# A decoder layer's mixer: diagonal and lowest HGRN scores by products and ones matmuls, narrow stationary operands at level 64, and mLSTM score matmuls of two heads in turn

## The chip, the cores and the metric

The kernel runs on one core of a Trainium2 chip. Its parts here are TensorE (PE in the profile; PEld is its weight load), VectorE (DVE), ScalarE (ACT), GpSimd (POOL) and SyncE (SP, which issues the DMAs). The metric is the time of one execution in device microseconds. Before the change it is 960.95 us, the median of 3 runs (960.86 to 961.06).

## The reference

One decoder layer on 512 tokens of width 1024, in float32: a SwiGLU feed-forward block, a token mixer, and a second SwiGLU block, each between RMS norms with a residual. The mixer has four HGRN2 heads (128 wide) and four mLSTM heads (q and k 64 wide, values 128 wide). The part that this change touches is how scores are formed.

```
# HGRN, per head: G is the running sum of log f, k = 1 - f
scores[t, s] = sum_d q[t, d] * k[s, d] * exp(G[t, d] - G[s, d])      for s <= t
o = scores @ v + (q * exp(G)) @ state
# mLSTM, per head
P[t, s] = (q[t] . k[s]) * exp(D[t, s] - m[t])                         for s <= t
```

On the diagonal (s = t) the HGRN decay is 1 and the score is sum_d q k. For neighbours (t odd, s = t - 1) it is sum_d q[t] f[t] k[s], because one step of decay is f[t] = 1 - k[t].

## The kernel before, in words

Activations lie transposed, features on partitions and tokens along the free axis, so a matmul contracts over features. Precision comes from splitting each float32 operand in a high and a low part in the fp32r format and adding three products (hi·hi, hi·lo, lo·hi): lines L126 to L128, L433, L443 and L488 are these dense products. ScalarE makes the high part of each weight block (`split`, L208), VectorE the low part (L210). Four such blocks stand ready ahead of TensorE (`WBUF`), and each load of a raw block waits until an earlier one has been split.

The mixer lies between about 360 and 640 us. Its small score matmuls are float32 and stand between pieces of the big projections: `fill(n)` takes n pieces from a list of jobs (six 256-column matmuls of `job_f`, or three 512-column matmuls of `job_t`), so that TensorE has work while ScalarE and VectorE prepare the next operands. Instructions of each engine run in the order in which they were placed; that order is fixed when the program is built.

HGRN heads are handled in two pairs (p = 0, 1). Within blocks of 128 tokens the scores are formed by levels: at level c (64, 32, 16, 8, 4, 2, 1) a block of 2c tokens is cut in half, rows of the later half are multiplied with columns of the earlier half, both scaled with decays taken from the token at the cut. `hgrn_level` makes qe and ke on VectorE (L995, L996, L1003) and ScalarE (L997, L998), does 8 matmuls with 128 stationary and 64 moving columns (L1008), and writes the masked part of the result into the score tile sT (L1012, a predicated copy on VectorE). The lowest level, c = 1, needs no exponential: qe is q times 1 - k (L1000, L1003), and the stationary operand is k itself. `hgrn_diag` forms the diagonal from 8 matmuls of 128 by 128 (L1048), of which one entry in 128 is kept by a predicated copy through an identity mask (L1050). `hgrn_levels` sets the order: lowest level and diagonal first, then `hgrn_decays` (L956 to L968, which overwrites k by G - ln k), then the levels from 64 down. The matmul at L1008 for level 64 therefore comes after k has been overwritten and exponentiated.

`mlstm_scores` runs over the four mLSTM heads. For each, a matmul with a selector of 36 rows (L1148, `neg_m`) spreads the running maximum over the partitions, VectorE and ScalarE form the exponent (L1170 to L1173), GpSimd cuts it to the causal part, and four matmuls (L1182) of 64 rows form q·k. Heads 0 and 2 lie in partitions 0 to 63 of their tile, heads 1 and 3 in partitions 64 to 127. L1184 multiplies the two.

A float32 matmul shows as two rows of PE and two of PEld in the profile: the 8 matmuls of a level are 16 loads.

Names in the tile list that matter below: `st` is a ring of four 128x512 tiles shared by qe, el, e and others; `gpre` and `gpost` are 128x1024 tiles that hold the gains of the norms, loaded by SP when free; `xn` is a 128x1024 tile used in turn for several things; `ps` are the eight PSUM banks.

Of the kernel before, what the change touches and what calls it, by code (L numbers as in the profile page):

```python
# [67 lines left out]
class Layer:  # L68
# [814 lines left out]
    def masks(self, mc, mb):  # L883

        nc = self.nc

        self.mask = mb.tile([P, len(LEVELS), 64], I32, name="mask")
        nc.gpsimd.memset(self.mask, 1)
        for n, c in enumerate(LEVELS):
            m = self.mask[:, n, :].rearrange("p (b c) -> p b c", c=c)  # L890
            pat = [[-2 * c, 64 // c], [0, c]]
            nc.gpsimd.affine_select(m, m, pattern=pat, compare_op=ALU.is_ge, fill=0.0, base=0, channel_multiplier=1)
            pat = [[2 * c, 64 // c], [0, c]]
            nc.gpsimd.affine_select(m, m, pattern=pat, compare_op=ALU.is_ge, fill=0.0, base=c - 1, channel_multiplier=-1)
        self.eye = mb.tile([P, P], I32, name="eye")
        nc.gpsimd.memset(self.eye, 1)
        nc.gpsimd.affine_select(
            self.eye, self.eye, pattern=[[1, P]], compare_op=ALU.is_equal, fill=0.0, base=0, channel_multiplier=-1
        )

        sel = mb.tile([4, 6, 2, 64], F32, tag="tmp", bufs=1, name="sel")
        nc.gpsimd.memset(sel, 1.0)
        self.sel = mc.tile([36, 6, P], F32R, name="selr")
        nc.gpsimd.memset(self.sel.bitcast(I32), 0)
        for n in range(6):
            pat = [[0, 2], [0, 64]] if n < 4 else [[-1, 2], [0, 64]]
            base = -n if n < 4 else -2 * (n - 4)
            nc.gpsimd.affine_select(
                sel[:, n], sel[:, n], pattern=pat, compare_op=ALU.is_equal, fill=0.0, base=base, channel_multiplier=1
            )  # L910
        for r in (0, 32):
            nc.gpsimd.tensor_copy(self.sel[r : r + 4], sel.rearrange("p n a b -> p n (a b)"))
# [32 lines left out]
            self.G.append(G)  # L945
            self.fill(4)

    def st(self, name, n=512):
        return self.sp.tile([P, n], F32, tag="st", bufs=4, name=self.nm(name))

    def hgrn_decays(self, p):

        nc = self.nc
        G, H = self.G[p], self.kk[p]

        nc.scalar.activation(H, H, AF.Ln, bias=self.tiny)  # L956
        nc.vector.tensor_tensor(H, G, H, op=ALU.subtract)
        chunks = lambda t: t.rearrange("p a (c t) -> p (a c) t", c=NT)
# [7 lines left out]
        d = self.sp.tile([P, 2, T], F32, tag="xn", bufs=1, name=self.nm("ek"))  # L966
        nc.vector.tensor_tensor(chunks(d), end.broadcast_to([P, 8, P]), chunks(H), op=ALU.subtract)
        nc.scalar.activation(d, d, AF.Exp)  # L968
        return d

    def hgrn_edges(self, p, d):
# [4 lines left out]
        for a in range(2):  # L976
# [2 lines left out]
                nc.tensor.transpose(pt[:, c * P : (c + 1) * P], d[:, a, c * P : (c + 1) * P], self.ident)  # L979
            nc.scalar.copy(self.kdt[:, 2 * p + a, :], pt[:, : 3 * P])  # L980

    def hgrn_level(self, p, n, ke):

        nc = self.nc
        c = LEVELS[n]
        q, kk, G = self.q[p], self.kk[p], self.G[p]
        flat = lambda t: t.rearrange("p a t -> p (a t)")
        blk = lambda t: flat(t).rearrange("p (b two c) -> p b two c", two=2, c=c)
        qe = self.st("qe")
        qe3 = qe.rearrange("p (b c) -> p b c", c=c)  # L990
        if c > 1:
            el = self.st("el")
            el3 = el.rearrange("p (b c) -> p b c", c=c)
            ref = blk(G)[:, :, 0, c - 1 : c].broadcast_to([P, 512 // c, c])
            nc.vector.tensor_tensor(qe3, blk(G)[:, :, 1, :], ref, op=ALU.subtract)  # L995
            nc.vector.tensor_tensor(el3, ref, blk(kk)[:, :, 0, :], op=ALU.subtract)  # L996
            nc.scalar.activation(qe, qe, AF.Exp)  # L997
            nc.scalar.activation(blk(ke)[:, :, 0, :], el3, AF.Exp)  # L998
        else:
            nc.vector.tensor_scalar(qe3, blk(kk)[:, :, 1, :], -1.0, 1.0, op0=ALU.mult, op1=ALU.add)  # L1000
            ke = kk
        yield
        nc.vector.tensor_tensor(qe3, qe3, blk(q)[:, :, 1, :], op=ALU.mult)  # L1003
        yield
        sc = self.ps()
        k8, q8 = flat(ke).rearrange("p (n s) -> p n s", s=P), qe.rearrange("p (n u) -> p n u", u=64)
        for m in range(8):
            nc.tensor.matmul(sc[:, 64 * m : 64 * m + 64], k8[:, m], q8[:, m], start=True, stop=True)  # L1008
        yield
        so = self.sT[:, 8 * p : 8 * p + 8, :].rearrange("p n (b two c) -> p n b two c", two=2, c=c)[:, :, :, 1, :]  # L1010
        mk = self.mask[:, n : n + 1, :].broadcast_to([P, 8, 64]).rearrange("p n (b c) -> p n b c", c=c)
        nc.vector.copy_predicated(so, mk, sc.rearrange("p (n b c) -> p n b c", n=8, c=c))  # L1012
        yield

    def hgrn_levels(self, p, kes, per, then=lambda: None):

        L = [self.hgrn_level(p, n, kes[n % 2]) for n in range(len(LEVELS))]
        N = len(L)
        next(L[0])
        next(L[0])  # L1020
        self.hgrn_diag(p)
        self.fill(per // 2)
        next(L[0])
        d = self.hgrn_decays(p)
        self.fill(per // 2)
        next(L[1])
        next(L[0])
        self.fill(per)
        for n in range(1, N):
            if n == 2:  # L1030
                self.hgrn_edges(p, d)
                then()
            if n + 1 < N:
                next(L[n + 1])
            next(L[n])
            if n > 1:
                next(L[n - 1])
            self.fill(per)
            next(L[n])
        next(L[N - 1])  # L1040

    def hgrn_diag(self, p):
        nc = self.nc
        for a in range(2):
            sc = self.ps()
            for c in range(NT):
                s = slice(c * P, (c + 1) * P)
                nc.tensor.matmul(sc[:, s], self.kk[p][:, a, s], self.q[p][:, a, s], start=True, stop=True)  # L1048
            h = 2 * p + a
            nc.vector.copy_predicated(  # L1050
                self.sT[:, 4 * h : 4 * h + 4, :], self.eye[:, None, :].broadcast_to([P, NT, P]), sc.rearrange("p (n s) -> p n s", s=P)
            )

    def hgrn_states(self):

# [107 lines left out]
    def mlstm_head(self, h):  # L1163

        nc = self.nc
        nm = self.neg_m(h)
        nm4 = nm.rearrange("p (c t) -> p c t", c=NT)
        e = self.st("e")
        e4 = e.rearrange("p (c t) -> p c t", c=NT)
        nc.vector.tensor_tensor(e4, nm4, self.aT[:, :, h : h + 1].broadcast_to([P, NT, P]), op=ALU.add)  # L1170
        nc.vector.tensor_copy(self.nend[:, h, :].rearrange("p (c o) -> p c o", o=1), nm4[:, :, P - 1 : P])
        nc.vector.tensor_scalar(e, e, 0.0, None, op0=ALU.min)
        nc.scalar.activation(e, e, AF.Exp)  # L1173
        nc.gpsimd.affine_select(
            e4, e4, pattern=[[0, NT], [1, P]], compare_op=ALU.is_ge, fill=0.0, base=0, channel_multiplier=-1
        )
        yield
        o = 64 * (h % 2)
        sc = self.ps()
        for c in range(NT):  # L1180
            s = slice(c * P, (c + 1) * P)
            nc.tensor.matmul(sc[:, s], self.qk[o : o + 64, 2 + h // 2, s], self.qk[o : o + 64, h // 2, s], start=True, stop=True)  # L1182
        yield
        nc.vector.scalar_tensor_tensor(self.pT[:, h, :], sc, 0.125, e, op0=ALU.mult, op1=ALU.mult)  # L1184
        yield

    def mlstm_scores(self, mc):

        nc = self.nc
        self.nend = mc.tile([P, NH, NT], F32, name="nend")  # L1190
        self.pT = mc.tile([P, NH, T], F32, name="pT")
        H = [self.mlstm_head(h) for h in range(NH)]
# [8 lines left out]
        nc.vector.tensor_tensor(w, self.aT, self.nend.rearrange("p h c -> p c h"), op=ALU.add)  # L1201
        nc.scalar.activation(w, w, AF.Exp)
# [6 lines left out]
        for p in range(2):  # L1209
            nm = self.neg_m(4 + p)  # L1210
# [17 lines left out]
            for c in range(3):  # L1228
# [5 lines left out]
                op=ALU.mult,  # L1234
# [3 lines left out]
        for c in range(3):  # L1238
            for p in range(2):
# [267 lines left out]
```

## Time and profile before

| what | number |
|---|---|
| median of 3 runs | 960.95 us |
| span of the profiled execution | 959.3 us |
| between the two | 1.65 us |
| granted TensorE clock, mean | 0.998 |
| TensorE busy | 950.6 us, 99% |
| VectorE, ScalarE, GpSimd busy | 711.6, 464.0, 291.2 us |
| score matmuls of levels 64 to 2 (L1008) | 22.7 us, 192 rows |
| score matmuls of level 1 (L1008, stationary kk) | 3.8 us, 32 rows |
| diagonal (L1048) | 3.9 us, 32 rows |
| mLSTM scores (L1182) | 4.6 us, 32 rows |
| a load of a gain tile (gpre), from issue to landing | 4.1 us |

The span is from the first to the last instruction of the profiled execution; it is 0.2% under the median of the runs, which have a start and an end around it. Times of a row are microseconds from the start of the span. A row of the list in order of time has its start, the busy time, the engine, the line, the operation and what it writes and reads; equal rows that follow one another are merged with a count. The start of one weight load to the start of the next is the best measure of TensorE's pace, since the ends of matmuls are modelled.

### The profile page before, as it was taken

How to read it: one execution, taken by the hardware profiler on the slowest of the kernel's cores; microseconds unless marked ns; L12 is line 12 of the kernel's file. 1: busy time of each engine (PE TensorE's matmuls, PEld its weight loads, DVE VectorE, ACT ScalarE, POOL GpSimd, SP SyncE). 2: the span in 40 equal slices, each digit the busy share in tenths (PEclk: the TensorE clock that was granted, in tenths of full speed). 3: DMA queues.
4: the chain of work that ended last, by engine and by line, in shares of the span. 5: the costliest groups of instructions: out<-in, count | busy, mean ns of one | idle time of the engine just before them, and what ended most of it. 6: DMA issues, size and time to landing. Idle time of an engine off the chain costs nothing.

```text
span 959.3 us, 15957 instructions
## 1 busy us (share of the span) xinstructions
PE 950.6 (99%) x6587; PEld 875.3 (91%) x6587; DVE 711.6 (74%) x796; ACT 464.0 (48%) x625; POOL 291.2 (30%) x224
## 2 busy tenths in 40 slices
PE   9999999999999999999999999999999999999997
PEld 7999999999888889998887888899999999988885
DVE  6898999998444476697846565797899999853543
ACT  7645454445434356855632444664444444543531
POOL 2546555651000035200001310354555575100001
PEclk9999999999999999999999999999999999999999
DMA  9243343335222024321312124314333333233202
GB/s 318 79 133 113 108 127 117 110 102 184 88 95 82 1 75 127 109 67 45 87 45 67 44 89 152 101 56 132 111 111 105 120 113 104 95 105 109 88 1 87
DMA packets 81667, 95.97 MB, mean 100 GB/s; under 512 B 4118, under 2 KB 61498, under 8 KB 81595
## 3 DMA queue, kind: packets, MB, share of 16 engines
q1 hardware_dynamic: 81306, 94.44, 31.6%
q8 instruction: 51, 0.84, 0.4%
q10 hardware_dynamic: 288, 0.52, 0.2%
q14 instruction: 22, 0.17, 0.1%
HBM read 92.85 MB, written 2.10 MB: 99 GB/s over the span
## 4 chain that ended last, share of the span: by engine, by line
PE 97%; DMA 1%; issue 1%; ACT 0%; POOL 0%; DVE 0%; SPq 0%; DVEq 0%; POOLq 0%; ACTq 0%
PE ps L488 45%; PE ps L126 13%; PE ps L128 13%; PE ps L127 13%; PE ps L433 6%; PE ps L1008 3%; PE ps L267 1%; PE ps L443 1%; DMA xs<-in_x_dram 1%; PE ps L1182 0%; PE ps L1093 0%; PE ps L1289 0%; PE ps L1262 0%; PE ps L1048 0%; PE ps L1286 0%
## 5 line engine op out<-in xcount | busy, mean ns | idle before, releaser
L210 DVE TENSOR_TENSOR w<-raw,w 128x1024 fp32r<-128x1024 f32 x214 | 364.4, 1710 | 125.7 <-ACT w L208 125.7
L208 ACT CAST w<-raw 128x1024 fp32r<-128x1024 f32 x214 | 224.0, 1053 | 321.7 <-PE ps L128 118.4
L222 POOL TENSOR_TENSOR raw<-raw,raw 128x1024 f32<-128x1024 f32 x80 | 221.0, 2764 | 170.7 <-DVE w L210 160.2
L488 PE MATMUL ps<-xq,w 128*128 128x256 f32 x2016 | 238.1, 277 | 0.0
L488 PEld LDWEIGHTS ps<-xq,w 128*128 128x128 f32 x2016 | 233.7, 188 | 0.2
L488 PE MATMUL ps<-sq,w 128*128 128x256 f32 x1440 | 171.0, 277 | 0.0
L488 PEld LDWEIGHTS ps<-sq,w 128*128 128x128 f32 x1440 | 167.4, 188 | 0.0
L128 PE MATMUL ps<-w,hs 128*128 128x512 f32 x336 | 131.0, 390 | 0.0
L126 PE MATMUL ps<-w,hs 128*128 128x512 f32 x336 | 130.9, 390 | 0.0
L127 PE MATMUL ps<-w,hs 128*128 128x512 f32 x336 | 130.8, 389 | 0.0
L126 PE MATMUL ps<-w,xq 128*128 128x512 f32 x208 | 84.9, 408 | 0.1
L128 PE MATMUL ps<-w,xq 128*128 128x512 f32 x208 | 81.1, 391 | 0.0
L127 PE MATMUL ps<-w,xq 128*128 128x512 f32 x208 | 81.0, 390 | 0.0
L128 PEld LDWEIGHTS ps<-w,hs 128*128 128x128 f32 x336 | 63.1, 188 | 13.8 <-DVE hs L672 0.7
L126 PEld LDWEIGHTS ps<-w,hs 128*128 128x128 f32 x336 | 63.1, 188 | 12.9
L127 PEld LDWEIGHTS ps<-w,hs 128*128 128x128 f32 x336 | 63.1, 188 | 12.7
L354 POOL TENSOR_SCALAR col<-col 128x1 f32<-128x1 f32 x24 | 9.5, 394 | 203.8 <-ACT junk L353 203.7
L433 PE MATMUL ps<-xq,w 128*128 128x256 f32 x480 | 56.5, 279 | 0.0
L433 PEld LDWEIGHTS ps<-xq,w 128*128 128x128 f32 x480 | 55.5, 188 | 0.0
L672 DVE TENSOR_TENSOR hs<-hf,hs 128x1024 fp32r<-128x1024 f32 x42 | 51.1, 1217 | 0.0
L128 PEld LDWEIGHTS ps<-w,xq 128*128 128x128 f32 x208 | 39.0, 188 | 8.9 <-DVE xq L274 0.3
L126 PEld LDWEIGHTS ps<-w,xq 128*128 128x128 f32 x208 | 39.1, 188 | 8.6 <-ACT xq L273 0.7
(230 smaller groups left out, 975.0 us busy)
## 6 DMA issues: line engine op xcount, KB each, us to landing
raw<-in_ffn_w_in_dram SPq DMA_DIRECT2D x88, 512.0 KB, 4.3
raw<-in_ffn_w_out_dram SPq DMA_DIRECT2D x44, 512.0 KB, 3.8
raw<-in_w_mix_in_dram SPq DMA_DIRECT2D x28, 512.0 KB, 3.9
raw<-in_w_mix_out_dram SPq DMA_DIRECT2D x8, 512.0 KB, 3.6
out_dram<-xs SPq DMA_DIRECT2D x8, 256.0 KB, 2.1
xs<-in_x_dram SPq DMA_DIRECT2D x6, 256.0 KB, 7.4
gpost<-in_norm_post_dram SPq DMA_DIRECT2D x3, 512.0 KB
gpre<-in_norm_pre_dram SPq DMA_DIRECT2D x2, 512.0 KB, 4.1
```

Of the source, the lines that this page charges most:

```text
L126: mm(ps, sh, mh, start=start, stop=False, **kw)
L127: mm(ps, sh, ml, start=False, stop=False, **kw)
L128: mm(ps, sl, mh, start=False, stop=stop, **kw)
L208: nc.scalar.copy(hi, raw)
L210: nc.vector.tensor_tensor(lo, raw, hi.bitcast(F32), op=ALU.subtract)
L222: nc.gpsimd.tensor_tensor(o, o, c, op=ALU.add)
L267: self.nc.tensor.transpose(pt[:, c * P : (c + 1) * P], src[:, k * P : (k + 1) * P], self.ident)
L433: mm(ps[:, u0:u1], w[:, a, k, :], self.xop(k, b, u0, u1), start=k + n + m == 0, stop=k == ND - 1 and n == 2, skip_group_check=True,)
L443: self.nc.tensor.matmul(ps[:, :HALF], w[:, a, k, :], self.xop(k, b, 0, HALF), start=m + k == 0, stop=m == 2 and k == ND - 1)
L488: self.nc.tensor.matmul(ps[:, c], wb[b][:, k, v], left[d][:, k, :], start=first and a + n + k == 0, stop=n == 2 and k == KH - 1, skip_grou ...
L672: self.nc.vector.tensor_tensor(t[:, 1], src, t[:, 0].bitcast(F32), op=ALU.subtract)
L1008: nc.tensor.matmul(sc[:, 64 * m : 64 * m + 64], k8[:, m], q8[:, m], start=True, stop=True)
```

## The change

Three edits, all in the mixer.

1. The 8 diagonal matmuls and the 8 matmuls of the lowest level of a pair go. `hgrn_lowest` forms the products on VectorE instead: `one` = q·k for both heads, and `near` = (q - q·k)·k of the token before, for every second token. Each is split in a high part (a copy on ScalarE) and a low part (a subtraction on VectorE), and six fp32r matmuls of 512 columns with a stationary matrix of ones sum them over the partitions. The sums stand in all 128 rows, and the same predicated copies as before pick what belongs in sT. The high and low parts of `one` are put in the gpre and gpost tiles, `near` and its parts in three of the four `st` tiles. The matrix of ones is made once by GpSimd. The six matmuls stand after the first `fill`, where the matmuls of the lowest level stood; the diagonal's place, ahead of that `fill`, is empty.
2. At level 64 only the first 64 of each 128 stationary columns are used, the result has 64 rows, and it is written by a copy on ScalarE without a mask (`put`).
3. mLSTM heads go in pairs: the matmuls of heads 0 and 1 alternate, then those of heads 2 and 3, into two banks each.

```
+        self.ones = mb.tile([P, P], F32R, name="ones")
+        nc.gpsimd.tensor_copy(self.ones, self.one.broadcast_to([P, P]))
...
+    def hgrn_lowest(self, p):
...
+        hi, lo = (by_a(self.cp.tile([P, D], F32R, tag=tag, bufs=1, name=self.nm(tag))) for tag in ("gpre", "gpost"))
+        one = self.sp.tile([P, 2, T], F32, tag="xn", bufs=1, name=self.nm("one"))
+        near, nhi, nlo = self.st("near"), self.st("nhi", dt=F32R), self.st("nlo", dt=F32R)
+        nc.vector.tensor_tensor(one, q, kk, op=ALU.mult)
+        nc.scalar.copy(hi, one)
+        nc.vector.tensor_tensor(near, by2(q)[:, :, 1], by2(one)[:, :, 1], op=ALU.subtract)
+        nc.vector.tensor_tensor(near, near, by2(kk)[:, :, 0], op=ALU.mult)
+        nc.scalar.copy(nhi, near)
+        yield
+        nc.vector.tensor_tensor(lo, one, hi.bitcast(F32), op=ALU.subtract)
+        nc.vector.tensor_tensor(nlo, near, nhi.bitcast(F32), op=ALU.subtract)
+        yield
+        scs = []
+        for ops in ((hi[:, 0], lo[:, 0]), (hi[:, 1], lo[:, 1]), (nhi, nlo)):
+            sc = self.ps()
+            for n, m in enumerate(ops):
+                nc.tensor.matmul(sc, self.ones, m, start=n == 0, stop=n == 1)
+            scs.append(sc)
+        yield
+        for a in range(2):
+            h = 2 * p + a
+            nc.vector.copy_predicated(
+                self.sT[:, 4 * h : 4 * h + 4, :], self.eye[:, None, :].broadcast_to([P, NT, P]),
+                scs[a].rearrange("p (n s) -> p n s", s=P),
+            )
+        self.put(p, 0, scs[2])
...
+    def put(self, p, n, sc):
...
+        if c == 64:
+            self.nc.scalar.copy(so[:64, :, 0], sc[:64].rearrange("p (n c) -> p n c", n=8))
+            return
...
-        if c > 1:
...
-        else:
-            nc.vector.tensor_scalar(qe3, blk(kk)[:, :, 1, :], -1.0, 1.0, op0=ALU.mult, op1=ALU.add)
-            ke = kk
...
+        r = 64 if c == 64 else P
         for m in range(8):
-            nc.tensor.matmul(sc[:, 64 * m : 64 * m + 64], k8[:, m], q8[:, m], start=True, stop=True)
+            nc.tensor.matmul(sc[:r, 64 * m : 64 * m + 64], k8[:, m, :r], q8[:, m], start=True, stop=True)
...
-        L = [self.hgrn_level(p, n, kes[n % 2]) for n in range(len(LEVELS))]
+        L = [self.hgrn_lowest(p)] + [self.hgrn_level(p, n, kes[n % 2]) for n in range(1, len(LEVELS))]
         N = len(L)
         next(L[0])
         next(L[0])
-        self.hgrn_diag(p)
         self.fill(per // 2)
...
-        o = 64 * (h % 2)
-        sc = self.ps()
+        scs = [self.ps(), self.ps()]
         for c in range(NT):
             s = slice(c * P, (c + 1) * P)
-            nc.tensor.matmul(sc[:, s], self.qk[o : o + 64, 2 + h // 2, s], self.qk[o : o + 64, h // 2, s], start=True, stop=True)
+            for a in range(2):
+                o = slice(64 * a, 64 * a + 64)
+                nc.tensor.matmul(scs[a][:, s], self.qk[o, 2 + p, s], self.qk[o, p, s], start=True, stop=True)
...
+        H = [self.mlstm_pair(p) for p in range(2)]
         next(H[0])
-        for h in range(NH):
-            if h + 1 < NH:
-                next(H[h + 1])
-            self.fill(3)
-            next(H[h])
-            next(H[h])
+        next(H[0])
+        self.fill(3)
+        next(H[1])
+        self.fill(3)
+        next(H[0])
+        next(H[0])
+        next(H[1])
+        self.fill(6)
+        next(H[1])
+        next(H[1])
```

More of the change, by code (lines that the diff above doesn't have):

```diff
@@ L946, in forget_gates, with st @@
             self.fill(4)
-    def st(self, name, n=512):
-        return self.sp.tile([P, n], F32, tag="st", bufs=4, name=self.nm(name))
+    def st(self, name, n=512, dt=F32):
+        return self.sp.tile([P, n], dt, tag="st", bufs=4, name=self.nm(name))
     def hgrn_decays(self, p):
@@ L1040, in hgrn_levels @@
         next(L[N - 1])
-    def hgrn_diag(self, p):
-        nc = self.nc
-        for a in range(2):
-            sc = self.ps()
[L1046 to L1052, printed above, removed]
     def hgrn_states(self):
@@ L1161, in conv, with mlstm_pair @@
             nc.vector.scalar_tensor_tensor(y[:, s:], x[:, : T - s], tap(j), y[:, s:], op0=ALU.mult, op1=ALU.add)
-    def mlstm_head(self, h):
+    def mlstm_pair(self, p):
         nc = self.nc
[L1166 to L1177, printed above, removed]
-        o = 64 * (h % 2)
-        sc = self.ps()
+        es = []
+        for h in (2 * p, 2 * p + 1):
+            nm = self.neg_m(h)
+            nm4 = nm.rearrange("p (c t) -> p c t", c=NT)
+            e = self.st("e")
+            e4 = e.rearrange("p (c t) -> p c t", c=NT)
+            nc.vector.tensor_tensor(e4, nm4, self.aT[:, :, h : h + 1].broadcast_to([P, NT, P]), op=ALU.add)
+            nc.vector.tensor_copy(self.nend[:, h, :].rearrange("p (c o) -> p c o", o=1), nm4[:, :, P - 1 : P])
+            nc.vector.tensor_scalar(e, e, 0.0, None, op0=ALU.min)
+            nc.scalar.activation(e, e, AF.Exp)
+            nc.gpsimd.affine_select(
+                e4, e4, pattern=[[0, NT], [1, P]], compare_op=ALU.is_ge, fill=0.0, base=0, channel_multiplier=-1
+            )
+            es.append(e)
+            yield
+        scs = [self.ps(), self.ps()]
         for c in range(NT):
             s = slice(c * P, (c + 1) * P)
-            nc.tensor.matmul(sc[:, s], self.qk[o : o + 64, 2 + h // 2, s], self.qk[o : o + 64, h // 2, s], start=True, stop=True)
+            for a in range(2):
+                o = slice(64 * a, 64 * a + 64)
+                nc.tensor.matmul(scs[a][:, s], self.qk[o, 2 + p, s], self.qk[o, p, s], start=True, stop=True)
         yield
-        nc.vector.scalar_tensor_tensor(self.pT[:, h, :], sc, 0.125, e, op0=ALU.mult, op1=ALU.mult)
+        for a in range(2):
+            nc.vector.scalar_tensor_tensor(self.pT[:, 2 * p + a, :], scs[a], 0.125, es[a], op0=ALU.mult, op1=ALU.mult)
         yield
```

29 lines of the change are left out of this document (18 added, 11 removed).

## The prediction

> **What bounds the kernel now.** I read the page's totals first, then the chain that ended last, then TensorE's own waits.
>
> ```profile
> span 959.3 us, 15957 instructions
> PE 950.6 (99%) x6587; PEld 875.3 (91%) x6587; DVE 711.6 (74%) x796; ACT 464.0 (48%) x625; POOL 291.2 (30%) x224
> ...
> PE 97%; DMA 1%; issue 1%; ACT 0%; POOL 0%; DVE 0%; SPq 0%; DVEq 0%; POOLq 0%; ACTq 0%
> ```
>
> ```profile
> PE ps L122 <- POOL ident masks.py:199: 1.5, 1, 1.5
> ```
>
> TensorE is busy 99% of the span, the chain lies on it for 97%, and its longest wait is 1.5 us at the start. So an instruction taken off TensorE shortens the kernel by its place in TensorE's queue, and one that VectorE or ScalarE gains costs nothing until TensorE has to wait for it. The question is therefore twofold: TensorE's account, and whether the new operands come in time. The groups by shape give the rows concerned, a stretch of the mixer shows how full the others are.
>
> ```profile
> L1048 PE MATMUL ps<-q,kk 128*128 128x128 f32 x32 | 3.9, 275 | 0.0
> L1008 PE MATMUL ps<-qe,kk 128*128 128x64 f32 x32 | 3.8, 271 | 0.0
> ```
>
> ```profile
> 402.00:440.00 38.00, 38.00 (x315) 37.27 (x314) 33.64 (x49) 23.86 (x30) 0.00 (x0) 1.00 0.25 70
> ```
>
> The columns after the length are busy us of PE, PEld, DVE, ACT and POOL. VectorE has 38.00 - 33.64 = 4.4 us free there.
>
> **Diagonal and lowest level, on TensorE.** The weight loads in order of time give the pace.
>
> ```profile
> 396.84 1.86 PEld L1048 LDWEIGHTS ps<-q,kk 128*128 128x128 f32 x16
> 398.62 2.19 PEld L433 LDWEIGHTS ps<-xq,w 128*128 128x128 f32 x18
> 400.74 1.87 PEld L1008 LDWEIGHTS ps<-qe,kk 128*128 128x128 f32 x16
> ```
>
> ```profile
> 461.14 0.19 PEld L128 LDWEIGHTS ps<-w,xq 128*128 128x128 f32 x1
> ...
> 463.86 0.19 PEld L128 LDWEIGHTS ps<-w,xq 128*128 128x128 f32 x1
> 464.08 1.98 PEld L1008 LDWEIGHTS ps<-qe,ke 128*128 128x128 f32 x16
> ```
>
> The diagonal's 16 loads hold TensorE from 396.84 to 398.62, 1.78 us or 0.111 each; the lowest level's 16 have the same pace (3.8 against 3.9 us in the groups). Two blocks in two pairs are 4 x 1.78 = 7.1 us removed. Added are 12 fp32r matmuls of 512 columns. Between the two L128 rows lie 12 such matmuls in 2.72 us, 0.227 each, so 2.7 us. Net **-4.4 us**, 2.2 for each pair.
>
> **The same part, whether the products come in time.** Pair 0: q's second head is ready at 390.82.
>
> ```profile
> 390.22 0.60 ACT L1363 ACTIVATE q<-ps 128x512 f32<-128x512 f32 x1
> ...
> 392.88 1.04 ACT L208 CAST w<-raw 128x1024 fp32r<-128x1024 f32 x1
> ...
> 395.23 0.60 ACT L1363 ACTIVATE q<-ps 128x512 f32<-128x512 f32 x1
> ```
>
> ```profile
> 390.85 0.69 DVE L1003 TENSOR_TENSOR qe<-qe,q 128x512 f32<-128x512 f32 x1 [0.68 <-ACT q L1363]
> 393.01 0.96 DVE L975 TENSOR_TENSOR qd<-q,qd 128x768 f32<-128x768 f32 x1 [1.47 <-ACT qd L962]
> 393.95 1.22 DVE L210 TENSOR_TENSOR w<-raw,w 128x1024 fp32r<-128x1024 f32 x1
> ```
>
> In the changed program's order VectorE does `one` (1.22, as L210), the two steps of `near` (0.69 each; L1003 here already reads every second token at 0.69), qd (0.96) and a weight split (1.22): 390.85 + 4.8 = 395.6. Then comes `lo`, which needs the copy `hi`; ScalarE has that behind the third head's q, so from 395.83 for 1.04, to 396.9. `lo` ends at 398.1, `nlo` at 398.8. TensorE, without the diagonal, does its 18 filler matmuls from 396.84 (0.118 each: 18 lie between 398.62 and 400.74) and asks for `hi` at 399.0, for `lo` at 399.2. It is covered with 1 us to spare; each us later than that is a us of stall.
>
> Pair 1's products are made some 6 us before TensorE asks for them, but the next thing is closer. VectorE has in order, behind the gate's L1116, the steps that lead to level 64.
>
> ```profile
> 445.00 0.68 DVE L1116 SCALAR_TENSOR_TENSOR z<-z 4x512 f32<-4x512 f32 x1 [0.72 <-ACT z L1114]
> ...
> 447.67 1.22 DVE L1117 TENSOR_TENSOR_SCAN rowt<-one,z 4x512 f32<-4x512 f32 x1
> ...
> 461.19 1.22 DVE L210 TENSOR_TENSOR w<-raw,w 128x1024 fp32r<-128x1024 f32 x1
> ```
>
> L1116 follows, through ScalarE, a weight cast that waits for TensorE to free a block, so it moves with TensorE: 445.0 less the 2.6 us gained by then (2.2 and half of level 64's part, below), 442.4. From L1117 to the last exponent before L210 is 13.5 us of work now. The changed order has the same work there, plus L1116 itself, `nlo`, two qe, one el, the final multiply (0.69 each) and one more split (1.22): 5.3 us, less about 0.1 of overlap at ten places. The multiply, before far ahead, now stands last and ends at 442.4 + 13.5 + 4.4 = 460.3. TensorE comes to level 64 at 464.08 - 4.8 = 459.3 and to its first matmul 0.2 later. **+0.8 us** of stall (0 to 2.5: the walk's overlaps on one side, ScalarE's copies coming late on the other). Below it each level has 15 x 0.227 + 1.78 = 5.2 us of TensorE against four VectorE steps of about 0.7 and a split of 1.22, so it is not repeated.
>
> Costed at nothing: GpSimd's matrix of ones, made once, long before 399 (GpSimd is busy 30% of the span); ScalarE's extra copies (pair 0's are in the walk; pair 1's fall in the stretch above, where it is busy 23.86 of 38 us); the predicated copies, as many as before but for level 64, whose eviction moves to ScalarE and frees 0.7 us of VectorE. The gain tiles are used until pair 1's ones matmuls, so SP's two gain loads move from before the mixer to just behind these, ahead of a weight load that waits for a VectorE split in any case; their readers come at the mixer's end. Uncovered, each would cost its landing.
>
> **Level 64.** Sixteen loads of 64 columns instead of 128, per pair. The load's length goes with its columns:
>
> ```profile
> L1008 PEld LDWEIGHTS ps<-qe,ke x192: 187/192/193, 413.1 to 493.4; 128*128 128x128 f32 x192
> ```
>
> ```profile
> L1093 PEld LDWEIGHTS ps<-xq,gw x32: 163/164/166, 428.8 to 432.5; 128*100 128x100 f32 x32
> ```
>
> 28 columns less are 24 to 28 ns less, so 64 less may take 0.055 to 0.064 us off 0.111. The shortest pace in the trace is that of eight 4-row loads:
>
> ```profile
> 466.79 0.13 PEld L1136 LDWEIGHTS ps<-ident,z 4*128 4x128 f32 x1 [0.17 <-issue]
> ...
> 467.22 0.14 PEld L1137 LDWEIGHTS ps<-ident,z 4*128 4x128 f32 x1
> ```
>
> 0.43 / 7 = 0.061. I take 0.060. But a 64-column operand is another tiling of the array than the matmuls around it, and the mLSTM block shows what such a step costs:
>
> ```profile
> 509.79 0.19 PEld L128 LDWEIGHTS ps<-w,xq 128*128 128x128 f32 x1
> 510.33 0.96 PEld L1182 LDWEIGHTS ps<-qk 64*128 64x128 f32 x8 [0.35 <-DVE w L1201]
> ...
> 511.52 0.19 PEld L127 LDWEIGHTS ps<-w,xq 128*128 128x128 f32 x1
> ```
>
> From L128 to L127 are 1.73 us; two ordinary steps are 0.45 and eight loads 0.89, which leaves 0.39 for going in and out. Level 64 then takes 16 x 0.060 + 0.39 = 1.35 instead of 1.78: **-0.9 us** for both pairs (bounds: no shorter pace at 0.111, +0.8; pace 0.050, -1.2). The Trainium skill (TensorEngine Tiling, Key Properties) says that changing the tiling mode drains TensorE; the 0.35 us idle above agrees, and by that rule alone the edit loses. The skill (TensorE: Matmul & The Clock Gate, LDWEIGHTS) has the load take its columns / 1.2 ns, 53 ns for 64; by it the estimate would be -1.1 us for both.
>
> **mLSTM.** Before, TensorE goes six times into the 64-row tiling; the changed order has five visits, -0.39. Whether the alternation helps shows where a selector load of rows 0 to 63 meets head 1's in rows 64 to 127:
>
> ```profile
> 506.98 0.74 PEld L1182 LDWEIGHTS ps<-qk 64*128 64x128 f32 x6 [0.35 <-issue]
> 507.53 0.18 PEld L1148 LDWEIGHTS ps<-nm,selr 36*128 36x128 f32 x1
> 507.64 0.30 PEld L1182 LDWEIGHTS ps<-qk 64*128 64x128 f32 x2
> ```
>
> The sixth L1182 load begins at 506.98 + 5 x 0.111 = 507.53, with L1148's, and the seventh at 507.64 on its own pace: two row groups work at once. Then 32 loads take the place of 16, -1.78; two selector matmuls that were hidden so are no longer, +0.45. Together -1.7; with some skew between the heads I take **-1.5 us** (no overlap: +0.1).
>
> **Sum.** -4.4 + 0.8 - 0.9 - 1.5 = -6.0 us. The profiled span is 959.3, the median 1.65 above; the same difference on the median gives 954.95, rounded to 955.0 us.
>
> **Rivals.** *Level 64 does not pay*: the pace stays at 0.111 and the step costs 0.39; 1.7 us less gain, 956.7. For: no load under 100 columns of this kind is in the trace. Against: 192 against 164 ns. *The heads do not overlap*: 1.6 us less, 956.6. For: the one overlap seen is of a float32 and an fp32r matmul. *The products hold TensorE up*: VectorE and ScalarE work in order, and pair 0's `lo` stands behind a copy that waits for ScalarE's third q, at 1 us of slack. With `lo` at 398.1 + 1.0 of slack + 6.0 = 405.1 us the whole gain is gone, from 407.0 on the kernel is slower by over 0.2%; at 409 it takes 964.9. Against: that is 9 us beyond the walk's 398.1, when the walk itself is 8 us long. *The change does not do what it says*, since stalls at pair 0 or at pair 1's level 64 take back 4 to 8 us: 959.0 to 962.9. For: VectorE's 89% in 402 to 440. Against: the change adds there pair 1's `one`, `lo` and `near`, 2 x 1.22 + 2 x 0.69 = 3.8 us, and takes away a multiply and a predicated copy of about 0.7 each, which fits into the free 4.4.
>
> **How the numbers follow.** 0.2% of 960.95, about what a measurement can tell, is 1.9 us. Chances: the sum as it stands 0.55, level 64 not paying 0.18, no overlap 0.15, nothing measurable 0.06, slower by the products 0.06. The first three are faster: 0.88. Without the stall and with the better ends (-4.4 - 1.2 - 1.7) it is 953.6; with both middle rivals 958.3. The range 953.2 to 958.3 leaves out the last two cases and a little at each end.
>
> **What would show it.** Right: L1048 gone, 12 rows of 512 columns at 0.227; level 64's loads near 134 ns at 0.06; mLSTM's 16 loads of a pair in about 0.9 us; a TensorE gap under 2.5 us ahead of pair 1's level 64, none ahead of pair 0's ones matmuls. Wrong: a gap at the latter, level 64's block at 1.8 us or more, or mLSTM's at 1.8.

## The result and the profile after

The changed kernel takes 954.5 us, the median of five runs (954.05 to 955.48), against 960.95 (960.29 to 961.34) for the kernel before: 0.9936 of it, with a 95% interval of 0.9924 to 0.9948. The prediction was 955.0 with a range of 953.2 to 958.3. A second set of five runs gave 954.57.

The totals of the page and its chain, then the one of TensorE's waits over 0.2 us that is new (total, times, longest):

```profile
span 952.5 us, 15862 instructions
PE 942.9 (99%) x6535; PEld 867.0 (91%) x6535; DVE 716.2 (75%) x800; ACT 464.7 (49%) x628; POOL 291.3 (31%) x225
...
PE 96%; DVE 2%; issue 1%; ACT 1%; POOL 0%; DVEq 0%; POOLq 0%; ACTq 0%
```

```profile
PE ps L1052 <- ACT ke L1044: 0.8, 1, 0.8
```

TensorE lost 7.7 us of busy time and the span 6.8 us. What TensorE saved and the span did not is 0.9 us; 0.8 of it is this wait. The chain that ended last now leaves TensorE for some 20 us ahead of it (VectorE's 2%, and ScalarE's 1%). TensorE still bounds the kernel.

The groups by shape that answer to L1048 and to level 1's L1008 (now L1007, the ones matmuls: this group, four more rows that read gpost, and two each that read nhi and nlo, 12 in all), to level 64 and to L1182 (now L1215):

```profile
L1007 PE MATMUL ps<-gpre,ones 128*128 128x512 f32 x4 | 1.6, 396 | 0.0
...
L1052 PE MATMUL ps<-qe,ke 128*64 128x64 f32 x32 | 2.3, 224 | 0.8 <-ACT ke L1044 0.8
...
L1215 PE MATMUL ps<-qk 64*128 64x128 f32 x32 | 2.3, 285 | 0.0
```

L1048 and the 32 rows of level 1 are gone. The mLSTM scores are 2.3 us of PE instead of 4.6, with as many rows: two run at a time.

To place the gain I count time from one row that lies ahead of everything in the mixer, four transposes near 360 us. The kernels differ there by up to 0.8 us (359.64 to 360.41 over the traces of the two tables below) although nothing ahead of it has to do with the edits, so clock times of two traces are not compared directly.

```profile
360.41 0.42 PEld L267 LDWEIGHTS ps<-ident,hf 128*128 128x128 f32 x4
...
413.12 1.87 PEld L1008 LDWEIGHTS ps<-qe,ke 128*128 128x128 f32 x16
...
419.64 1.86 PEld L1008 LDWEIGHTS ps<-qe,ke 128*128 128x128 f32 x16
...
470.69 1.98 PEld L1008 LDWEIGHTS ps<-qe,ke 128*128 128x128 f32 x16
...
500.49 0.29 PEld L1148 LDWEIGHTS ps<-nm,selr 36*128 36x128 f32 x2 [0.35 <-issue]
...
514.77 0.31 PEld L1229 LDWEIGHTS ps<-ident,qk 128*128 128x128 f32 x3
```

```profile
359.84 0.42 PEld L267 LDWEIGHTS ps<-ident,hf 128*128 128x128 f32 x4
...
410.11 1.01 PEld L1052 LDWEIGHTS ps<-qe,ke 128*64 128x64 f32 x16
...
416.03 1.87 PEld L1052 LDWEIGHTS ps<-qe,ke 128*128 128x128 f32 x16
...
459.49 1.01 PEld L1052 LDWEIGHTS ps<-qe,ke 128*64 128x64 f32 x16 [1.19 <-ACT ke L1044]
465.31 1.98 PEld L1052 LDWEIGHTS ps<-qe,ke 128*128 128x128 f32 x16
...
495.11 0.29 PEld L1177 LDWEIGHTS ps<-nm,selr 36*128 36x128 f32 x2 [0.35 <-issue]
...
507.65 0.31 PEld L1267 LDWEIGHTS ps<-ident,qk 128*128 128x128 f32 x3 [0.25 <-PE ps L1215]
```

The first fence is the kernel before, the second the changed one; the columns are start, length, operation and count of the weight loads, and the last row of each is the first load behind the mLSTM scores. Counted from the first row of each (level 64 of pair 1 before is the row at 464.08 that the prediction shows):

| start of | before | after | gained so far |
|---|---|---|---|
| pair 0, level 64 | 52.71 | 50.27 | 2.44 |
| pair 0, level 32 | 59.23 | 56.19 | 3.04 |
| pair 1, level 64 | 103.67 | 99.65 | 4.02 |
| pair 1, level 32 | 110.28 | 105.47 | 4.81 |
| mLSTM, first selector load | 140.08 | 135.27 | 4.81 |
| behind the mLSTM scores | 154.36 | 147.81 | 6.55 |
| end of the span | 598.89 | 592.66 | 6.23 |

So 4.8 us come from the HGRN levels, 1.7 from the mLSTM scores, and nothing moves between the two. Behind them 0.3 is given back, at one place: an L126 load near 584 us sits idle for 0.67 us until ScalarE's xq (L273) is there, where in the kernel before (at 591.24) it was 0.39.

### The profile page after: what moved, and what is told of

Its sections match the earlier page's. It is cut to its first block, busy times and chain, and to the rows that moved or that the text cites. A ratio compares the mean times of both kernels' runs of the same rounds, so it can differ in the third digit from the quotient of the medians.

```text
span 952.5 us, 15862 instructions
## 1 busy us (share of the span) xinstructions
PE 942.9 (99%) x6535; PEld 867.0 (91%) x6535; DVE 716.2 (75%) x800; ACT 464.7 (49%) x628; POOL 291.3 (31%) x225
## 4 chain that ended last, share of the span: by engine, by line
PE 96%; DVE 2%; issue 1%; ACT 1%; POOL 0%; DVEq 0%; POOLq 0%; ACTq 0%
PE ps L488 45%; PE ps L126 12%; PE ps L128 12%; PE ps L127 12%; PE ps L433 6%; PE ps L1052 2%; PE ps L267 1%; PE ps L443 1%; PE ps L1122 0%; PE ps L115 0%; PE ps L122 0%; PE ps L1327 0%; PE ps L1300 0%; PE ps L1324 0%; PE ps L1089 0%
## 5 line engine op out<-in xcount | busy, mean ns | idle before, releaser
L128 PE MATMUL ps<-w,hs 128*128 128x512 f32 x336 | 131.0, 390 | 0.0
L126 PE MATMUL ps<-w,hs 128*128 128x512 f32 x336 | 130.9, 390 | 0.0
L126 PE MATMUL ps<-w,xq 128*128 128x512 f32 x208 | 84.7, 407 | 0.3 <-ACT xq L273 0.2
L128 PE MATMUL ps<-w,xq 128*128 128x512 f32 x208 | 81.1, 391 | 0.0
L128 PEld LDWEIGHTS ps<-w,hs 128*128 128x128 f32 x336 | 63.1, 188 | 13.8 <-DVE hs L672 0.7
L126 PEld LDWEIGHTS ps<-w,hs 128*128 128x128 f32 x336 | 63.1, 188 | 12.8
L126 PEld LDWEIGHTS ps<-w,xq 128*128 128x128 f32 x208 | 39.1, 188 | 9.1 <-ACT xq L273 1.0
L128 PEld LDWEIGHTS ps<-w,xq 128*128 128x128 f32 x208 | 39.0, 188 | 8.9 <-DVE xq L274 0.3
```

The costliest lines, as they stand in the source:

```text
L126: mm(ps, sh, mh, start=start, stop=False, **kw)
L128: mm(ps, sl, mh, start=False, stop=stop, **kw)
```

## The experiments

Every kernel below computes the whole result. The same places for each, counted from its own row of transposes (the names are those of the sections below):

| start of | products only | products, multiply first | wide level 64 | copy on VectorE | changed | multiply first | heads in turn | heads as before |
|---|---|---|---|---|---|---|---|---|
| pair 0, level 64 | 50.07 | 50.07 | 50.08 | 50.27 | 50.27 | 50.27 | 50.28 | 50.27 |
| pair 0, level 32 | 56.70 | 56.70 | 56.71 | 56.18 | 56.19 | 56.19 | 56.20 | 56.19 |
| pair 1, level 64 | 100.85 | 99.00 | 100.86 | 100.33 | 99.65 | 98.81 | 99.65 | 99.63 |
| pair 1, level 32 | 107.39 | 105.61 | 107.38 | 106.11 | 105.47 | 104.58 | 105.47 | 105.42 |
| mLSTM, first selector | 137.19 | 135.41 | 137.18 | 135.91 | 135.27 | 134.38 | 135.27 | 135.22 |
| behind the mLSTM scores | 151.46 | 149.69 | 149.73 | 148.45 | 147.81 | 146.93 | 148.46 | 149.49 |
| end of the span | 595.98 | 594.25 | 594.31 | 593.02 | 592.66 | 591.78 | 593.23 | 594.36 |

### Products only

Edits 2 and 3 are undone; the diagonal and the lowest level stay as products.

```
-        if c == 64:
-            self.nc.scalar.copy(so[:64, :, 0], sc[:64].rearrange("p (n c) -> p n c", n=8))
-            return
...
-        r = 64 if c == 64 else P
+        r = P
...
-        H = [self.mlstm_pair(p) for p in range(2)]
+        H = [self.mlstm_head(h) for h in range(NH)]
```

> Part 1 alone: diagonal and lowest level by products and ones matmuls; level 64 and the mLSTM heads as in the kernel before. Theory (4.4 us off TensorE, 0.8 us given back as a wait ahead of pair 1's level 64): 3.6 us faster than before, 957.3 us, ratio 0.9962. Rival (the products' cost on VectorE is hidden everywhere): 4.4 us, 956.5 us, ratio 0.9954.

957.59 us (957.21 to 957.76), 0.9966 of before, interval 0.9953 to 0.9978: 3.3 us gained, near the 3.6 of the count less its stall, and 1.1 short of the count alone. TensorE's new wait is longer here, 1.5 us at pair 1's level 64:

```profile
PE ps L1049 <- ACT ke L1041: 1.5, 1, 1.5
```

### VectorE's last multiply first

In `hgrn_levels` the multiply of level 64 goes ahead of the next level's subtractions.

```
+            if n == 1:
+                next(L[n])
             if n + 1 < N:
                 next(L[n + 1])
-            next(L[n])
+            if n > 1:
+                next(L[n])
```

On the changed kernel:

> The changed kernel with level 64's last multiply placed ahead of level 32's exponents, in both pairs. Theory (TensorE waits at pair 1's level 64 for that multiply, which stands behind other VectorE work): the multiply ends some 3 us earlier, ahead of TensorE, the gap of about 1 us goes, 953.5 us, ratio 0.9925. Rival (the wait is for ScalarE's exponential of ke, as the profile puts it down): the gap stays, 954.5 us, ratio 0.9935.

953.67 us (953.47 to 953.93), 0.9925 of before, interval 0.9912 to 0.9939. The wait is gone from the list, and level 64 starts at 98.81 instead of 99.65. The median is 0.8 to 0.9 below the two sets of the changed kernel, and the table has the same gain, 0.84 at level 64. VectorE and the load of it:

```profile
455.48 0.69 DVE L1046 TENSOR_TENSOR qe<-qe,q 128x512 f32<-128x512 f32 x1
```

```profile
458.93 1.01 PEld L1052 LDWEIGHTS ps<-qe,ke 128*64 128x64 f32 x16 [0.35 <-issue]
```

The multiply is done at 456.17, 2.8 us ahead of the load. So the wait was for VectorE's multiply, although the list of waits of the changed kernel names ScalarE's ke. Its rows show how that comes about (ScalarE, then VectorE):

```profile
454.08 0.63 ACT L1044 ACTIVATE ke<-el 128x512 f32<-128x512 f32 x1
...
458.80 0.63 ACT L1044 ACTIVATE ke<-el 128x512 f32<-128x512 f32 x1 [1.08 <-DVE el L1042]
```

```profile
458.67 0.71 DVE L1046 TENSOR_TENSOR qe<-qe,q 128x512 f32<-128x512 f32 x1
```

Level 64's own ke was done at 454.71. The instruction that ends at 459.43, just ahead of the load at 459.49, is the ke of level 32, which has the same line. What the load needs is the multiply that ends at 459.38.

The same order on the products alone:

> Only the diagonal and lowest level by products, and VectorE's last multiply ahead of pair 1's level 64 placed before the next level's subtractions. The products alone took 957.6, 3.3 below the kernel before, with a wait of 1.5 us at that place. Theory: part 1 is worth the 4.4 us of its count of loads less that wait; without it 956.2 to 956.5, and no wait over 0.3 us at that level. Rival: part 1 is worth 3.3 by itself and the wait is covered elsewhere: 957.6 again.

955.99 us (955.66 to 956.84), 0.9951, interval 0.9937 to 0.9965: 1.6 us under the products alone, and no wait but the one at the start is left. Part 1 without its wait gains 598.89 - 594.25 = 4.64 us from the row of transposes to the end. That is a little more than the count of 4.4. The rest, 0.26, lies in the filler loads between the lowest level and level 64 of pair 0, 90 in both kernels. From the first of them to level 64 it is 10.33 us here (399.99 to 410.32) and 10.59 before (402.53 to 413.12). Why they run closer is open.

### Wide level 64, and its copy on VectorE

Edit 2 is undone alone: 128 stationary columns, and the masked copy on VectorE as for the other levels.

```
-        if c == 64:
-            self.nc.scalar.copy(so[:64, :, 0], sc[:64].rearrange("p (n c) -> p n c", n=8))
-            return
...
-        r = 64 if c == 64 else P
+        r = P
```

> The changed kernel with 128 stationary columns at level 64 and the masked copy on VectorE, as before; parts 1 and 3 stay. Theory (a load takes time by its columns, a change of tiling costs 0.39 us): 0.9 us slower than the changed kernel, 955.4 us, ratio 0.9942; the 16 loads at 0.111 us each and no gap on either side. Rival (the drain eats it): 954.5 us or less. What it can't tell by the time alone, since 0.9 us is near its uncertainty, the loads in order of time will.

956.13 us (955.85 to 959.12), 0.9956, interval 0.9943 to 0.9968: edit 2 is worth 1.6 us, not 0.9. The loads of pair 0:

```profile
409.97 1.86 PEld L1049 LDWEIGHTS ps<-qe,ke 128*128 128x128 f32 x16
411.70 0.70 PEld L981 LDWEIGHTS ps<-ident,ek 128*128 128x128 f32 x6
```

```profile
411.19 0.64 PEld L981 LDWEIGHTS ps<-ident,ek 128*128 128x128 f32 x6
```

In the wide kernel the next operation starts 1.73 us after level 64's first load, in the changed kernel (second fence; level 64 at 410.11) 1.08 us. The table has the way in as well: the narrow loads start 0.2 us later (50.27 against 50.08). Net, one pair gains 0.5 (56.71 to 56.19 at level 32), both together 1.0, near the prediction's 0.9. The other part is in the wait, which is 0.8 in the changed kernel and 1.5 here, the same row as for the products only.

To part the two, the loads stay narrow and only the copy goes back to VectorE:

```
-        if c == 64:
-            self.nc.scalar.copy(so[:64, :, 0], sc[:64].rearrange("p (n c) -> p n c", n=8))
-            return
+        r = 64 if c == 64 else P
...
-        self.nc.vector.copy_predicated(so, mk, sc.rearrange("p (n b c) -> p n b c", n=8, c=c))
+        self.nc.vector.copy_predicated(so[:r], mk[:r], sc[:r].rearrange("p (n b c) -> p n b c", n=8, c=c))
```

> The changed kernel with level 64's result written by a masked copy of 64 rows on VectorE, in place of the plain copy on ScalarE; its narrow loads stay. The kernel with wide loads and VectorE's copy took 956.1, 1.6 above the changed one, and its own trace puts 0.9 of that on the loads and 0.7 on a longer wait at pair 1's level 64 (1.5 in place of 0.8). Theory: that 0.7 is the copy's, 0.7 us of VectorE in a stretch where VectorE runs without a break; then 955.2 here, loads of level 64 at 0.058, wait 1.5. Rival: the wait goes with the wide loads; then 954.5 and a wait of 0.8.

954.93 us (954.46 to 955.12), 0.9938, interval 0.9926 to 0.995. The wait goes with the copy, not with the loads:

```profile
PE ps L1050 <- ACT ke L1042: 1.5, 1, 1.5
```

From the row of transposes to the wait's end this kernel is 0.68 behind the changed one, to the mLSTM 0.64, behind its scores still 0.64, at the end 0.36; the medians have 0.4. It is not simply the copy's own 0.7 us that is passed on, since VectorE rests in between (1.25 us ahead of the last row of the first fence below). What differs is the order that was built. ScalarE and VectorE ahead of pair 1's gate, in this kernel and then in the changed one:

```profile
438.70 1.05 ACT L208 CAST w<-raw 128x1024 fp32r<-128x1024 f32 x1 [1.80 <-PE ps L128]
439.77 0.63 ACT L1140 ACTIVATE z<-z 4x512 f32<-4x512 f32 x1
...
443.03 0.68 DVE L1143 SCALAR_TENSOR_TENSOR z<-z 4x512 f32<-4x512 f32 x1 [1.25 <-ACT z L1141]
```

```profile
436.13 0.63 ACT L1142 ACTIVATE z<-z 4x512 f32<-4x512 f32 x1
438.37 1.05 ACT L208 CAST w<-raw 128x1024 fp32r<-128x1024 f32 x1 [1.62 <-PE ps L128]
...
441.39 0.68 DVE L1145 SCALAR_TENSOR_TENSOR z<-z 4x512 f32<-4x512 f32 x1 [0.72 <-ACT z L1143]
```

With the copy, ScalarE's first step of the gate stands behind the weight cast, which waits for TensorE; without it, ahead of the cast. VectorE's step that follows the gate starts at 443.03 - 360.18 = 82.85 from the transposes, against 441.39 - 359.84 = 81.55. Some of the work behind it has been done by then, so the last multiply ends only 0.7 later (460.39 against 459.38, 100.21 against 99.54). No run keeps the copy on VectorE with the other order, so that the 0.7 comes by way of the order rests on these rows. The 0.3 is given back at the L126 load named above, which sits idle for 0.39 us here (at 585.17) and 0.67 in the changed kernel. What sets this is open: with the copy on ScalarE it is 0.67 in most kernels, but 0.39 in the two with a late product below.

### Heads as before, and heads in turn

Edit 3 is undone alone:

```
-        H = [self.mlstm_pair(p) for p in range(2)]
+        H = [self.mlstm_head(h) for h in range(NH)]
```

> The changed kernel with the mLSTM heads as before, one at a time; parts 1 and 2 stay. Theory (two row groups of TensorE work at once, and one visit to the 64-row tiling is saved): 1.7 us slower than the changed kernel, 956.2 us, ratio to before 0.995; the mLSTM stage has six visits and 0.9 us for 8 loads of one head again. Rival (the alternation brings nothing, the gain came from elsewhere): 954.5 us, ratio 0.9935.

955.94 us (955.68 to 956.97), 0.9952, interval 0.994 to 0.9965: 1.4 above the changed kernel by the medians. In the table the scores, from the first selector to the row behind, take 149.49 - 135.22 = 14.27 us here and 12.54 in the changed kernel, and the end lies 1.70 later, the 1.7 of the theory.

Then the pairs stay, and only the alternation goes: head 0's four matmuls, then head 1's.

```
-        for c in range(NT):
-            s = slice(c * P, (c + 1) * P)
-            for a in range(2):
-                o = slice(64 * a, 64 * a + 64)
+        for a in range(2):
+            o = slice(64 * a, 64 * a + 64)
+            for c in range(NT):
+                s = slice(c * P, (c + 1) * P)
```

> The changed kernel with each mLSTM pair's 8 matmuls ordered as all four of one head, then all four of the other; the visits to the 64-row tiling are as in the changed kernel. Theory (the gain is the alternation): a pair's 16 loads take about 1.7 us instead of 0.9, 1.6 us in all, 956.1 us, ratio 0.995. Rival (the gain is that there are fewer visits and the banks are apart): 954.5 us, ratio 0.9935.

955.25 us (954.82 to 955.56), 0.9942, interval 0.9928 to 0.9955. Both theories miss: the loss is 0.7, under half of the 1.6 that serial loads would cost. The loads of the first pair, alternating (the changed kernel) and in turn:

```profile
500.71 0.97 PEld L1215 LDWEIGHTS ps<-qk 64*128 64x128 f32 x16 [0.35 <-DVE e L1203]
501.59 0.19 PEld L1177 LDWEIGHTS ps<-nm,selr 36*128 36x128 f32 x1
...
502.14 0.19 PEld L127 LDWEIGHTS ps<-w,xq 128*128 128x128 f32 x1
```

```profile
501.13 1.29 PEld L1215 LDWEIGHTS ps<-qk 64*128 64x128 f32 x14 [0.35 <-DVE e L1203]
502.24 0.18 PEld L1177 LDWEIGHTS ps<-nm,selr 36*128 36x128 f32 x1
502.35 0.30 PEld L1215 LDWEIGHTS ps<-qk 64*128 64x128 f32 x2
...
502.88 0.19 PEld L127 LDWEIGHTS ps<-w,xq 128*128 128x128 f32 x1
```

In turn, the whole block is 502.88 - 501.13 = 1.75 us, against 502.14 - 500.71 = 1.43. The last two loads begin at 502.35, 1.22 us after the first; on one pace of 0.111 the fifteenth would begin 1.55 us after it. So some of head 1's loads ran beside head 0's though the program has them behind, and the selector runs beside the tail. The scores of both pairs take 148.46 - 135.27 = 13.19 us here, between 12.54 and the 14.27 of the heads as before. So the alternation itself is worth 0.3 for each pair, 0.65 for two; the other 1.1 of edit 3's 1.7 goes with the pairing itself, which brings fewer visits and two row groups in one visit. No run parts these two.

### A late product

Pair 0's `lo` is computed three times over, then six times, to use up the slack that the prediction gave it.

```
+        if p == 0:
+            for _ in range(2):      # 5 in the second kernel
+                nc.vector.tensor_tensor(lo, one, hi.bitcast(F32), op=ALU.subtract)
```

> The changed kernel with pair 0's low part computed three times, so that the last one ends later. By VectorE's order it would end at about 400.9 us of the span instead of 397.5. Theory (about 1.2 us of slack, then each us late is a us of stall): a gap of 2.3 us ahead of the second ones matmul, 956.8 us, ratio 0.9957. Rival (TensorE finds other work or the delay is caught up later): 954.5 us, ratio 0.9935.

956.95 us (956.75 to 959.94), 0.9965, interval 0.9953 to 0.9978: 2.4 above the changed kernel, as expected. But the gap ahead of the ones matmuls is not the expected 2.3. TensorE's waits:

```profile
PE ps L1055 <- DVE qe L1049: 1.8, 1, 1.8
PE ps L1010 <- DVE gpost L1003: 1.7, 1, 1.7
```

1.7 us fall at the ones matmuls that read `lo`, and the wait at pair 1's level 64 grows from 0.8 to 1.8. The rows, counted from the transposes (at 359.72 here), show where the slack went: `lo` ends at 400.81, 3.47 later than in the changed kernel, and its first matmul loads at 400.87, 2.57 later, so 0.9 fell into the slack. The built order puts the three ones matmuls that do not need `lo` or `nlo` ahead of it, and TensorE reaches level 64 of pair 0 (411.97) 1.98 later.

> The same with pair 0's low part computed six times; the last one would end at about 407.2 us. Theory: a gap of 8.6 us, 963.1 us, slower than before, ratio 1.002. Rival A (caught up later, since the stages behind have slack on VectorE): under 960 us. Rival B (the long gap also lowers the granted clock for some us): 965 us or more, with a granted clock under 1.0 behind the gap.

962.11 us (960.9 to 964.22, 11 runs), 1.0017 of before, interval 1.0008 to 1.0026: the whole gain is gone, as the prediction's rival said, 1 us less dear than expected. But there is no gap of 8 us (in this trace the row of transposes stands at 361.69, 1.85 later than in the changed kernel):

```profile
400.97 6.19 PEld L433 LDWEIGHTS ps<-xq,w 128*128 128x128 f32 x51
...
409.11 0.30 PEld L1010 LDWEIGHTS ps<-gpost,ones 128*128 128x128 f32 x2 [1.95 <-DVE gpost L1003]
```

```profile
PE ps L1055 <- ACT cx L1187: 2.5, 1, 2.5
PE ps L1055 <- DVE qe L1049: 1.9, 1, 1.9
```

The built order puts 51 filler loads ahead of the two ones matmuls that read `lo`, so no more than the 1.95 of this row show there. More comes at the levels behind: 2.5 at level 32 of pair 0, whose load starts at 423.43, and 1.9 at pair 1's level 64, where the changed kernel waits 0.8. Three stretches, with the granted clock ahead of the last two columns (after the length stand PE, PEld, DVE, ACT and POOL):

```profile
408.00:410.00 2.00, 0.89 (x5) 0.80 (x6) 2.00 (x3) 0.61 (x2) 0.00 (x0) 1.00 0.62 236
420.00:424.00 4.00, 1.48 (x14) 1.30 (x13) 4.00 (x8) 3.35 (x7) 0.00 (x0) 1.00 0.47 131
424.50:427.90 3.40, 3.40 (x18) 3.40 (x18) 2.85 (x5) 0.72 (x2) 0.00 (x0) 0.50 0.00 0
```

In the gaps, the first two, the clock is 1.00, so there the loss is waiting. But behind the second it is halved for 3.4 us: TensorE is busy throughout, and level 32's 16 loads last 2.53 us instead of 1.87. Half of 3.4, an estimate of 1.7 us, is lost so in this run, which took 963.97. Rival B thus has the clock right and the time too high. The eleven runs go the same way: three with a mean clock of 0.999 took 960.9 to 961.3, three with 0.994 took 964.1 to 964.2. So the waits alone seem to use up the gain, and what lies above that goes in the main with the clock (the profiled run, at 0.997, has the 1.85 us ahead of the mixer as well).

The changed kernel once more, beside these:

> The changed kernel once more, beside the three others on the same chip: 954.5 us, ratio 0.9935.

954.57 us (953.89 to 954.76), 0.9933, interval 0.9921 to 0.9946.

## Why the prediction was right

**What bounds the kernel.** It held: TensorE's account, plus the places where an operand is late, gave 955.0 for a measured 954.5.

**Diagonal and lowest level, -4.4.** Measured 4.64 without the wait, of which 0.26 is the closer fillers that the count does not have. The ones matmuls of pair 0 keep the pace taken from L128, and stand behind the fillers without an idle time:

```profile
398.31 0.19 PEld L1007 LDWEIGHTS ps<-gpre,ones 128*128 128x128 f32 x1
398.42 0.19 PEld L1007 LDWEIGHTS ps<-gpost,ones 128*128 128x128 f32 x1
...
399.58 10.40 PEld L433 LDWEIGHTS ps<-xq,w 128*128 128x128 f32 x90
```

Six in 399.58 - 398.31 = 1.27 us, 0.21 each beside 0.227 predicted.

**Pair 0 in time, with 1 us to spare.** VectorE's rows, in order:

```profile
390.28 1.23 DVE L994 TENSOR_TENSOR one<-q,kk 128x1024 f32<-128x1024 f32 x1 [0.69 <-ACT q L1401]
391.54 1.20 DVE L996 TENSOR_TENSOR near<-q,one 128x512 f32<-128x512 f32 x1
...
396.23 1.23 DVE L1000 TENSOR_TENSOR gpost<-one,gpre 128x1024 fp32r<-128x1024 f32 x1 [0.76 <-ACT gpre L995]
```

`lo` ends at 397.46; its first matmul loads at 398.42, 1.0 us later. In the walk it was the same 1 us, with all times 0.6 later. As in the walk, `lo` waits for ScalarE's copy (the 0.76 ahead of it), not for VectorE. The first run with the late `lo` shows that the slack is real, 0.9 of its 3.47 us. That its 2.4 us of added VectorE work cost 2.4 in the medians is a coincidence: in the trace 2.0 fell at pair 0, 1.0 at pair 1's level 64, and 0.3 came back near 584.

**Pair 1's level 64, +0.8.** Measured 0.84 at the place (99.65 against 98.81 with the multiply first) and 0.88 at the end. The mechanism is the predicted one: the multiply stands last in VectorE's queue, and the walk from the gate's step to its end had 17.9 us where the trace has 459.38 - 441.39 = 17.99. The size is closer than its parts. Counted from the transposes the multiply ended at 99.54 (99.89 in the walk) and TensorE was there at 98.81 (98.89). That leaves 0.73, and the load followed 0.11 behind the multiply; the prediction had 1.0, less 0.2 for the first matmul.

**Level 64, -0.9.** With the multiply first on both sides, so that no wait covers it, the narrow kernel is ahead at level 32 of pair 1 by what the table has as 105.61 - 104.58 = 1.03. The 16 loads take (1.01 - 0.13) / 15 = 0.059 us each, beside 0.060 predicted, and their length is near the 134 ns:

```profile
L1052 PEld LDWEIGHTS ps<-qe,ke x192: 133/192/193, 410.1 to 488.0; 128*128 128x128 f32 x160, 128*64 128x64 f32 x32
```

Going in and out costs 0.2 (50.27 against 50.07) and 1.08 - 16 x 0.059 = 0.14, 0.34 together; the prediction took 0.39 from the mLSTM block. The 16 x (0.111 - 0.059) = 0.83 us saved on the loads outweigh the 0.34. The Trainium skill (TensorEngine Tiling (Array Packing), Key Properties) says that changing the tiling mode drains TensorE. The trace agrees as far as there is a price, these 0.34 us, and it is too small for the edit to lose.

**Costed at nothing: the eviction moved to ScalarE.** This term was mis-sized. The prediction counted 0.7 us of VectorE as freed and gave it no value. With the copy on VectorE the wait at pair 1's level 64 is 1.5, so the move is worth 0.7 there, and 0.4 of the total, by way of the order ahead of the gate as the rows have it. The 0.7 is inside the measured +0.84. The walk came out right without the term because it starts from the gate's row of the kernel before, where ScalarE's first step of the gate also stands ahead of the weight cast (438.79 and 441.97). Edit 2 alone was priced too low by it, the whole was not. Of the other terms put at nothing, no wait shows: from the load near 584 us to the end the two kernels keep their distance to 0.1 us.

**mLSTM, -1.5.** From the first selector load to the first load behind the scores are 514.77 - 500.49 = 14.28 us before and 507.65 - 495.11 = 12.54 after: 1.74. That is the whole count of 1.7. The 0.2 taken off for some skew between the heads was not needed. The 16 loads of a pair take 0.97 us (0.9 predicted). That the heads overlap because the matmuls alternate is half right: TensorE takes part of the second row group's loads ahead in any case.

**Behind the scores, nothing was predicted.** The load near 584 us gives back 0.67 - 0.39 = 0.28.

**Sum.** -4.64 + 0.84 - 1.03 - 1.74 + 0.28 = -6.29, beside 6.23 in the traces from the row of transposes (spans are given to 0.1), 6.45 in the medians and 6.0 predicted. The steps were off by 0.24, 0.04, 0.13 and 0.24, and the 0.28 was not seen; that the last two nearly cancel is luck. The range's lower end, 953.2, lies 0.4 under the best case of 953.6 that the prediction adds up, and no term of it gives that 0.4.

**The rivals.** Level 64 not paying (956.7) and no overlap (956.6) fell with the rows above. The products holding TensorE up was a true danger with the right sign: with `lo` computed six times the kernel is slower than before. `lo` ended at 409.06 in that trace, 47.37 behind the transposes, which is 407.8 by the clock of the kernel before. By the prediction's slack and one us of stall for each us later that gives 963.7. It took 962.1, since the built order moved fillers into the gap, and even of that a part goes with the halved clock, which the prediction does not have. Stalls of 4 to 8 us, the last rival, did not come: the one new stall is 0.84.

## What to carry to other kernels

Walk the queue of the helper engine to the place where TensorE meets it, and start the walk at the last point where that engine rested: an instruction that stands earlier there is worth the wait that it ends, 0.84 us here, and an edit elsewhere can be worth about as much (0.7 here) by changing the order in which the program is built. Where the list of waits names an instruction with the same line as one of the next round, look at which of the two had ended. A price for changing the tiling, 0.34 us here, is small beside 16 loads cut by half, and worth reckoning rather than avoiding. Where a change makes TensorE wait, look at the granted clock for some us behind the gap as well as in it. And count a stage from its own first row to the first row behind it: counted to the end of the span, the 1.74 of the mLSTM scores shows as 1.42.

## What the runs showed of the hardware that was not expected

Loads of the other row group run ahead without the program alternating them: 16 loads of two heads in turn took 1.22 us to the fifteenth, where one after the other would take 1.55.

Gaps of TensorE can be paid for twice. With `lo` six times, behind 4 us in which TensorE was busy 1.48, the granted clock was 0.50 for 3.4 us. With `lo` three times (waits of 1.7 and 1.8) the profiled run shows no such stretch in the mixer. These runs do not show how long a gap it takes.

VectorE's first step of `near` took 1.20 us in pair 0 and 0.69 in pair 1 (at 435.34), the same shape. In pair 0 GpSimd's cast of `selr` (L914) runs beside it, from 388.38 to 392.19, and takes 0.52 us longer than in the kernel before (3.81 against 3.29); the step takes 0.51 longer than its twin. That fits two operations that get in each other's way. Against it: `one`, beside the same cast, kept its 1.23, and in the kernel before the qe step at 390.85 kept its 0.69 beside it. No run took one of them away, so the cause is open. It cost nothing here, since VectorE sat idle for 0.76 us ahead of `lo` in any case.
